# Issuing all loads and stores of a batched matmul from one queue, each store four groups behind its loads

## The chip, the cores and the metric

The kernel runs on one core of one Trainium2 chip. The metric is the device time of the whole program in microseconds (us). Executions of a kernel before scatter by under 1%, so small differences are judged by means of several runs of the same rounds.

## The reference

```python
b1, b2, m, k, n = 8, 16, 256, 512, 384
x:      float32 [8, 16, 256, 512]
weight: float32 [8, 16, 512, 384]
out = np.matmul(x, weight)          # 128 independent 256x512 @ 512x384
```

168 MB are read and 50 MB written.

## The kernel before

The 128 batches are handled in groups: 63 groups of two batches and, at the end, two groups of one. A group loads one x tile (1 MiB; the last two groups share one) and one 768 KB weight tile per batch, casts both to bf16 on VectorE (DVE), transposes x on TensorE (PE), multiplies, copies PSUM to SBUF on ScalarE (ACT) and stores 768 KB. The last two groups store 384 KB each.

```python
LAG = 3
x_pool: bufs=3    w_pool: bufs=6    out_pool: bufs=LAG + 3

def load_x(b): ... nc.sync.dma_start(x_sb[:], ...)      # SP
def load_w(b): ... nc.sync.dma_start(w_sb[:], ...)      # SP

waiting = []
def store():
    dram, out_sb = waiting.pop(0)
    nc.scalar.dma_start(out=dram, in_=out_sb)           # ACT

for n, G in enumerate(groups):
    ...                                # loads, casts, transposes of group n
    if last:
        while waiting:
            store()
    for r in range(0, RG, 2):
        ...                            # matmuls into po
        nc.scalar.copy(out=out_sb[:, r : r + 2, :], in_=po[:, :, :N])
    waiting.append((..., out_sb))
    if len(waiting) > LAG or last:
        store()
```

Instructions reach each engine in an order that the framework's scheduler chooses. In this kernel it hoists each store on ACT to directly behind its own copies, whatever LAG says. Stores on SP keep the order of the source. Each transfer reports its landing on one of eight semaphores (counters that engines wait on), used in turn, and the program issues it only after the transfer eight before it has landed.

Of the kernel before, what the change touches and what calls it, by code (L numbers as in the profile page):

```python
# [1 line left out]

# [5 lines left out]


@with_exitstack
def kernel(
    ctx: ExitStack,
    tc: tile.TileContext,
    x: bass.AP,
    weight: bass.AP,
    out: bass.AP,
):
    nc = tc.nc
    P = 128  # L20

    b1, b2, M, K = x.shape
    _, _, _, N = weight.shape
    B = b1 * b2
    KO = K // P

    x_rows = x.rearrange("b1 b2 m k -> (b1 b2 m) k")
    o_rows = out.rearrange("b1 b2 m n -> (b1 b2 m) n")
    w_flat = weight.rearrange("b1 b2 k n -> (b1 b2) k n")

    fp32 = mybir.dt.float32
    bf16 = mybir.dt.bfloat16



    GX = 2
    CX = P // GX
    R = GX * M // P


    groups = [2] * ((B - GX) // 2) + [1] * GX

    LAG = 3

    const = ctx.enter_context(tc.tile_pool(name="const", bufs=1))
    x_pool = ctx.enter_context(tc.tile_pool(name="x_pool", bufs=3))
    xb_pool = ctx.enter_context(tc.tile_pool(name="xb_pool", bufs=2))
    xt_pool = ctx.enter_context(tc.tile_pool(name="xt_pool", bufs=2))
    w_pool = ctx.enter_context(tc.tile_pool(name="w_pool", bufs=6))
    wb_pool = ctx.enter_context(tc.tile_pool(name="wb_pool", bufs=4))  # L50
    out_pool = ctx.enter_context(tc.tile_pool(name="out_pool", bufs=LAG + 3))
    psum_t = ctx.enter_context(tc.tile_pool(name="psum_t", bufs=2, space=bass.MemoryType.PSUM))
    psum_o = ctx.enter_context(tc.tile_pool(name="psum_o", bufs=3, space=bass.MemoryType.PSUM))

    identity = const.tile([P, P], bf16)
    make_identity(nc, identity)

    def load_x(b):
        x_sb = x_pool.tile([P, R, K], fp32, name="x_sb")
        nc.sync.dma_start(  # L60
            x_sb[:], x_rows[b * M : (b + GX) * M].rearrange("(p r) k -> p r k", r=R)
        )
        return x_sb

    def load_w(b):
        w_sb = w_pool.tile([P, KO, N], fp32, name="w_sb")
        nc.sync.dma_start(w_sb[:], w_flat[b].rearrange("(kp ko) n -> kp ko n", ko=KO))  # L67
        return w_sb

    def transpose_x(x_sb, RG):  # L70


        H = R // RG
        x_bf = xb_pool.tile([P, R, K], bf16, name="x_bf")
        x_t = xt_pool.tile([P, RG, KO, P, H], bf16, name="x_t")
        for r0 in range(0, R, 4):
            nc.vector.tensor_copy(out=x_bf[:, r0 : r0 + 4], in_=x_sb[:, r0 : r0 + 4])  # L77
            for r in range(r0, r0 + 4, 2):
                pt = psum_t.tile([P, 2, KO, P], bf16, name="pt")
                for rr in range(2):  # L80
                    for ko in range(KO):
                        nc.tensor.transpose(  # L82
                            pt[:, rr, ko, :], x_bf[:, r + rr, ko::KO], identity
                        )
                j = r % RG
                nc.vector.tensor_copy(  # L86
                    out=x_t[:, j : j + 2, :, :, r // RG], in_=pt[:]
                )
        return x_t

    waiting = []

    def store():
        dram, out_sb = waiting.pop(0)
        nc.scalar.dma_start(out=dram, in_=out_sb)

    b = 0
    for n, G in enumerate(groups):
        last = n == len(groups) - 1
        C = P // G  # L100
        RG = G * M // P
        if b % GX == 0:
            x_sb = load_x(b)
        w_sb = [load_w(b + i) for i in range(G)]
        if b % GX == 0:
            x_t = transpose_x(x_sb, RG)
        w_bf = []
        for i in range(G):
            t = wb_pool.tile([P, KO, N], bf16, name="w_bf")
            nc.vector.tensor_copy(out=t[:], in_=w_sb[i][:])  # L110
            w_bf.append(t)
        if last:
            while waiting:
                store()

        out_full = out_pool.tile([P, 2 * M // P, N], fp32, name="out_sb")
        out_sb = out_full[:, :RG]
        for r in range(0, RG, 2):
            po = psum_o.tile([P, 2, 512], fp32, name="po")
            for rr in range(2):  # L120
                for ko in range(KO):
                    for i in range(G):
                        c0 = (b % GX + i) * CX
                        nc.tensor.matmul(  # L124
                            po[i * C : (i + 1) * C, rr, :N],
                            x_t[:, r + rr, ko, c0 : c0 + CX, :],
                            w_bf[i][:, ko, :],
                            start=(ko == 0),
                            stop=(ko == KO - 1),
                        )  # L130
            nc.scalar.copy(out=out_sb[:, r : r + 2, :], in_=po[:, :, :N])  # L131
        waiting.append(
            (
                o_rows[b * M : (b + G) * M].rearrange("(p r) n -> p r n", r=RG),
                out_sb,
            )
        )
        if len(waiting) > LAG or last:
            store()
        b += G  # L140


# [1 line left out]
_INS = ['x', 'weight']  # L144
_OUTS = [((8, 16, 256, 384), 'float32')]


# [23 lines left out]
```

## Time and profile before

| | before |
|---|---|
| time, median (four runs) | 531.7 us (531.2 to 532.2) |
| span of the profiled run | 528.1 us |
| chain that ended last | 97% DMA |
| both queues' share of 16 DMA engines | 76.4% + 23.0% |
| rate in 50 to 500 us | 422 GB/s |
| last weight tile's cast starts | 521.35 us |

The span runs from the first instruction to the last; the time adds some 2 us of start and end. The DMA engines are the bound, and they are full until about 510 us. What the end looks like is shown in the prediction.

### The profile page before, as it was taken

What the parts mean: (1) busy time and instruction counts of PE and PEld (TensorE: products, weight loads), DVE (VectorE), ACT (ScalarE), POOL (GpSimd) and SP (SyncE); (2) the same over time, 40 slices, a digit from 0 to 9 for tenths busy, and PEclk for the clock granted to TensorE, in tenths of its full rate; (3) what the DMA queues carried; (4) which work ended last, traced back from release to release, by engine and by line L of the source; (5) the groups of instructions that cost most, each with busy time, mean ns of one, the idle gap of its engine ahead of it and who ended that gap; (6) DMA issues with size and microseconds to landing.
All of it is one profiled execution on the core that took longest, in us unless ns stands there. A gap on an engine that the chain in (4) does not pass through costs nothing.

```text
span 528.1 us, 7363 instructions
## 1 busy us (share of the span) xinstructions
PE 343.7 (65%) x3056; PEld 234.3 (44%) x3056; DVE 277.9 (53%) x320; ACT 103.9 (20%) x129; POOL 0.7 (0%) x6
## 2 busy tenths in 40 slices
PE   4685566675766766676657667576575775766754
PEld 2454444443443544444434444354353443544432
DVE  4545545555465554555554555555555455455554
ACT  0212211221221212122112122121121211112212
POOL 0000000000000000000000000000000000000000
PEclk9969878888788887879888888898888788788889
DMA  8999999999999999999999999999999999999994
GB/s 343 399 427 422 425 421 420 427 418 423 423 419 425 421 422 424 421 423 423 421 423 421 421 424 421 422 424 422 423 419 424 422 423 422 422 422 424 422 414 192
DMA packets 37042, 218.59 MB, mean 414 GB/s; under 512 B 4113, under 2 KB 4113, under 8 KB 28817
## 3 DMA queue, kind: packets, MB, share of 16 engines
q1 hardware_dynamic: 27648, 167.78, 76.4%
q10 hardware_dynamic: 9360, 50.34, 23.0%
q8 instruction: 24, 0.39, 0.3%
q14 instruction: 10, 0.07, 0.0%
HBM read 167.77 MB, written 50.33 MB: 413 GB/s over the span
## 4 chain that ended last, share of the span: by engine, by line
DMA 97%; DVE 1%; PE 1%; issue 1%; SPq 0%; ACT 0%; DVEq 0%
DMA x_sb<-in_x_dram 97%; PE po L124 1%; DVE x_t L86 0%; DVE x_bf L77 0%; DVE w_bf L110 0%; SPq L60 0%; SPq L67 0%; ACT out_sb L131 0%; PE pt L82 0%; DVEq L77 0%
## 5 line engine op out<-in xcount | busy, mean ns | idle before, releaser
L124 PE MATMUL po<-w_bf,x_t 128*64 128x384 bf16 (+1 forms) x2032 | 276.4, 407 | 166.5 <-DVE w_bf L110 166.0
L124 PEld LDWEIGHTS <-x_t 128*64 128x64 bf16 (+1 forms) x2032 | 174.1, 135 | 252.6 <-DVE w_bf L110 127.6
L131 ACT COPY out_sb<-po 128x768 f32<-128x768 f32 x128 | 102.6, 802 | 420.2 <-PE po L124 415.9
L77 DVE CAST x_bf<-x_sb 128x2048 bf16<-128x2048 f32 x64 | 78.5, 1227 | 135.7 <-DMA x_sb<-in_x_dram 135.7
L110 DVE CAST w_bf<-w_sb 128x1536 bf16<-128x1536 f32 x128 | 119.8, 955 | 28.4 <-DMA w_sb<-in_weight_dram 27.9
L86 DVE COPY x_t<-pt 128x1024 bf16<-128x1024 bf16 x128 | 83.7, 696 | 80.3 <-PE pt L82 80.3
L82 PE MATMUL pt<-identity,x_bf 128*128 128x128 bf16 x1024 | 70.2, 222 | 13.8 <-DVE x_bf L77 13.6
L82 PEld LDWEIGHTS <-x_bf 128*128 128x128 bf16 x1024 | 60.1, 115 | 36.7 <-DVE x_bf L77 27.8
L131 ACT ACT_TABLE_LOAD x1 | 1.3, 1283 | 0.7 <-PEq L155 0.7
masks.py:199 POOL TENSOR_SCALAR_AFFINE_SELECT identity<-identity 128x128 bf16<-128x128 bf16 x1 | 0.3, 293 | 0.1
masks.py:197 POOL MEMSET identity<- 128x128 bf16 x1 | 0.2, 204 | 0.3 <-POOLq L155 0.3
L155 POOL MEMSET const-bfloat16-1.0<- 128x1 bf16 x1 | 0.1, 101 | 0.0
L155 POOL MEMSET const-uint8-127<- 128x1 uint8 x1 | 0.1, 101 | 0.0
L155 POOL MEMSET const-float32-0.0<- 128x1 f32 x1 | 0.1, 98 | 0.2 <-issue 0.2
L155 POOL MEMSET const-float32-1.0<- 128x1 f32 x1 | 0.1, 98 | 0.0
## 6 DMA issues: line engine op xcount, KB each, us to landing
w_sb<-in_weight_dram SPq DMA_DIRECT2D x128, 768.0 KB, 16.2
x_sb<-in_x_dram SPq DMA_DIRECT2D x64, 1024.0 KB, 16.1
out_dram<-out_sb ACTq DMA_DIRECT2D x63, 768.0 KB, 8.4
out_dram<-out_sb ACTq DMA_DIRECT2D x2, 384.0 KB, 2.3
```

What stands on the lines that cost most here:

```text
L77: nc.vector.tensor_copy(out=x_bf[:, r0 : r0 + 4], in_=x_sb[:, r0 : r0 + 4])
L82: nc.tensor.transpose(pt[:, rr, ko, :], x_bf[:, r + rr, ko::KO], identity)
L86: nc.vector.tensor_copy(out=x_t[:, j : j + 2, :, :, r // RG], in_=pt[:])
L110: nc.vector.tensor_copy(out=t[:], in_=w_sb[i][:])
L124: nc.tensor.matmul(po[i * C : (i + 1) * C, rr, :N], x_t[:, r + rr, ko, c0 : c0 + CX, :], w_bf[i][:, ko, :], start=(ko == 0), stop=(ko == K ...
L131: nc.scalar.copy(out=out_sb[:, r : r + 2, :], in_=po[:, :, :N])
L155: nc = _bacc.Bacc("TRN2", target_bir_lowering=False, num_devices=1)
```

## The change

Intent: one issuing queue with a fixed order in which the loads of a group always stand in front of the store of an earlier one, so that stores never overtake loads and enough stored work is left over to keep the DMA engines busy while the last group is computed.

```diff
-    LAG = 3
+    LAG = 4
...
-    def store():
+    def store(queue):
         dram, out_sb = waiting.pop(0)
-        nc.scalar.dma_start(out=dram, in_=out_sb)
+        queue.dma_start(out=dram, in_=out_sb)
...
         if last:
             while waiting:
-                store()
+                store(nc.sync)
...
         if len(waiting) > LAG or last:
-            store()
+            store(nc.sync)
```

`out_pool` grows from 6 to 7 buffers through `LAG + 3`.

## The prediction

> **What bounds the kernel now.** I read the page from the chain of waits outward: first what ended last, then whether that resource has any slack, then the two ends of the run, where slack can hide. The chain (part 4) leaves no doubt about the kind of bound:
>
> ```profile
> DMA 97%; DVE 1%; PE 1%; issue 1%; SPq 0%; ACT 0%; DVEq 0%
> ```
>
> 97% of the 528.1 us span is transfers. The other engines have room: PE is busy 65%, DVE 53%, ACT 20%. The queue part says how full the 16 DMA engines are, and how the two issuing queues share them:
>
> ```profile
> q1 hardware_dynamic: 27648, 167.78, 76.4%
> q10 hardware_dynamic: 9360, 50.34, 23.0%
> q8 instruction: 24, 0.39, 0.3%
> ```
>
> The columns are packets, MB and share of the time of 16 engines. q1 carries SP's loads, q10 ACT's stores. 76.4 + 23.0 + 0.3 = 99.7%. So two queues together fill the engines, and there is almost no gap for a new order to close. The windows view (us, busy time of five engines, granted clock, DMA share, GB/s) shows that this holds to about 510 us and no further:
>
> ```profile
> 50.00:500.00 450.00, 298.15 (x2665) 203.57 (x2665) 238.90 (x277) 88.63 (x111) 0.00 (x0) 0.85 1.02 422
> 510.00:515.00 5.00, 2.85 (x34) 1.86 (x32) 3.51 (x5) 0.80 (x1) 0.00 (x0) 1.00 0.95 397
> 515.00:520.00 5.00, 3.15 (x40) 2.37 (x36) 3.34 (x3) 1.60 (x2) 0.00 (x0) 1.00 0.69 279
> 520.00:525.00 5.00, 2.77 (x16) 1.48 (x16) 2.15 (x3) 1.60 (x2) 0.00 (x0) 1.00 0.29 114
> 525.00:528.10 3.10, 0.00 (x0) 0.00 (x0) 0.00 (x0) 0.00 (x0) 0.00 (x0) 0.77 0.45 178
> ```
>
> For 450 us the share is above 1 (packets of one engine overlap slightly) and the rate is 422 GB/s. Then 397, 279, 114: in the last 18 us the DMA engines run dry while the last group is computed. The timeline of ACT tells why:
>
> ```profile
> 517.10 0.80 ACT L131 COPY out_sb<-po 128x768 f32<-128x768 f32 x1 [0.50 <-PE po L124]
> 517.93 0.34 ACTq L95 DMA_DIRECT2D out_dram<-out_sb  x1
> 522.75 0.80 ACT L131 COPY out_sb<-po 128x768 f32<-128x768 f32 x1 [4.85 <-PE po L124]
> 523.58 0.34 ACTq L95 DMA_DIRECT2D out_dram<-out_sb  x1
> 524.05 0.80 ACT L131 COPY out_sb<-po 128x768 f32<-128x768 f32 x1 [0.50 <-PE po L124]
> 524.88 0.34 ACTq L95 DMA_DIRECT2D out_dram<-out_sb  x1
> ```
>
> Although the source says LAG = 3, the scheduled program issues each store directly after its own two copies (the same pattern stands at the first group: copies at 13.37 and 15.41, store at 16.24). So no stored work is left over for the end. When the last weight tile has landed (its cast starts at 521.35), nothing is queued behind it, and the last two half stores must wait for compute.
>
> **What the Trainium skill says.** "DMA: Bandwidth & Descriptors", section "Issuing engines are not separate DMA queues": transfers issued from different engines run on the same 16 DMA engines and interleave; a second issuer saves only issue time. The trace agrees: the shares above add to 99.7%, and an issue costs 0.33 us on SP. The same page, "Queues, rings and completion order": an engine takes turns between rows at packet granularity and consumes one ring in order. The trace agrees, in the time from issue to landing:
>
> ```profile
> w_sb<-in_weight_dram SPq DMA_DIRECT2D x128, 768.0 KB, 16.2
> x_sb<-in_x_dram SPq DMA_DIRECT2D x64, 1024.0 KB, 16.1
> out_dram<-out_sb ACTq DMA_DIRECT2D x63, 768.0 KB, 8.4
> ```
>
> A store on its own queue overtakes queued loads and lands in 8.4 us, a load in 16. "HBM Reference", "Specifications": a core streaming alone measures about 425 GB/s, bounded by its DMA engines; the trace has 422. Against the change, "Perfetto Trace Analysis", "DMA Optimizations", suggests one issuer for inputs and another for outputs where control flow is present; this program has no loop at run time, and nothing in the trace speaks for or against that.
>
> **The change, part by part.** No byte, copy or matmul changes. The built program has the 192 loads in the same order on SP, and the 65 stores move from ACT to SP, one behind each group's loads, starting after the loads of the fifth group. ACT keeps 128 copies.
>
> *Issue.* SP gains 65 issues of about 0.34 us = 22 us over 528 us; per group (8.25 us, 528/64) it then issues four transfers, 1.3 us. No bound. ACT loses the same 22 us and was 80% idle.
>
> *Steady state.* A transfer in this program waits until the one eight before it has landed (eight landing semaphores in turn). Four per group makes the window two groups: 2 x 3.25 MiB = 6.8 MB, at 422 GB/s 16.1 us. The window is as deep as before (six loads and two stores); only now all wait their turn in one ring, so stores should land in about 16 us instead of 8.4 and loads stay at about 16.
>
> *The new wait.* SP would stall if the store of group n-4 was not computed when its turn comes. Its turn comes when the store of group n-6 has landed, right after the last weight tile of group n-2, so two groups (16.5 us) after the last weight tile of group n-4 landed. From the last cast to the store issue the trace shows about 6.4 us (cast at 505.16, store at 511.49). Margin about 10 us, and behind it seven queued transfers. I expect zero stall from this, and none from the output buffers: group n reuses the buffer of group n-7, whose store landed more than a group earlier.
>
> *Packet rate.* In the packet records of the trace a 6144-byte packet takes a median of 234 ns as load and as store, an 8192-byte one 309 ns, whether the engines are doing loads alone or a mixture. Per engine: (16384 + 8064) x 234 ns + 8192 x 309 ns + small ones, over 16 = 520 us. That is the floor of any order. Before uses 2.05 us before the first packet, about 522 us of work on the slowest engine (slower first packets and instruction fetches make up the 2), and the rest is hole and drain.
>
> *The tail, the only place to gain.* By the packet records some engines still have loads until 521 us and all are then idle from about 522 to 524.4 us (2.4 us), with another 0.3 us between the two last half stores; the last packet ends at 526.9 and the span 1.3 us later. After the change, three full stores (1.87 us each: 786 KB at 422 GB/s) and the two half stores (0.93 each) lie behind the last weight load: 7.5 us of queued transfers. The last weight tile therefore lands about 516.5, and its compute (3.5 us from cast to last store issue, 521.35 to 524.88) plus 1.3 us to the first packet fits within the 5.6 us of the three full stores. The slowest engine then runs without a hole: 2.05 + 522 = 524.0 us, and 1.3 us of drain = 525.3 us of span, against 528.1: a gain of 2.8 us. Engines that already idled from 512 us on gain more, but the slowest one sets the end.
>
> Sum: -2.8 us (tail), 0 (steady state), up to +1 for bursts of stores alone (next paragraph), say +0.3. 532.1 - 2.5 = 529.6 us, which is 0.5% faster: within 2%.
>
> **Rivals.** (1) *Store bursts are slower than mixed traffic.* In one queue all engines do the same store at about the same time. For it: the 98 packets of stores that started with 15 or more stores and no loads active average 249 ns (median 236) against 234 to 235 in mixtures. If all 8064 store packets lost 15 ns, 8064 x 15 / 16 = 7.6 us, giving about 537. Against it: the outliers are few and the median is +2 ns (1 us). (2) *The end of each store holds the ring* until its writes are acknowledged, which the load queue filled until now. 65 x 0.2 us would be 13 us and about 542. Against it: in the first 13 us, with loads alone on one queue, the engines never idle between transfers; but that is no store. (3) *SP blocks on a store in order and the load queue drains.* Worth several per cent if it happened each group; the 10 us margin speaks against it. (4) *The engines' skew shrinks as well*: averaged over engines the idle time between 512 and 527 us is 5.7 us, so up to 3 us more gain, 526.5.
>
> **Range and chances.** The step I trust most is the full engines: nothing can gain over about 1.2%. The tail gain is solid but small; rivals 1 and 2 stretch the upper side. 526.5 to 533.5 us for 8 in 10. Faster by over 2% (below 521.5): 1%, since a span of some 519 us (the profiled run took 530.3 us for its 528.1 us of span) would undercut the packet floor. Slower by over 2% (above 542.8): 4%. Within: 95%.
>
> **What would show it.** Right: one hardware_dynamic queue of some 218 MB and about 99%; stores landing in about 16 us; SP waiting almost only for DMAs, not for ACT; 422 GB/s in 50 to 500 us; the rate staying near 420 up to a few us before the end. Wrong: a steady rate below 418 (rival 1 or 2, told apart by packet times against gaps), a wait of SP for out_sb of more than some us in sum (rival 3), or a hole before the last stores.

## More of the kernel before

The experiments ran in three sessions, each on another chip, so runs of two sessions are best compared by their ratios to the kernel before in their own session.

## The result, and the profile after

| | before | after |
|---|---|---|
| time, median of four runs each | 531.7 us | 526.88 us |
| span of the profiled run | 528.1 us | 524.1 us |
| ratio | | 0.9911 (95%: 0.989 to 0.9933) |

All ratios in this document are the mean time of one kernel's runs over that of the other's runs of the same rounds, so they are not quite the ratio of the medians quoted. The kernel is 0.9% faster, about 4.7 us: within 2% as predicted, and inside the range of 526.5 to 533.5, but at its lower edge (two of the four runs, 526.30 and 526.34, lie just below it, as does the 526.46 of a later repeat), and the gain is nearly twice the 2.5 us that was worked out.

The page after, its chain, its queues and its issues (size, median us to landing):

```profile
DMA 97%; PE 1%; DVE 1%; issue 0%; ACT 0%; SPq 0%; ACTq 0%; DVEq 0%
q1 hardware_dynamic: 37008, 218.12, 99.9%
q8 instruction: 24, 0.39, 0.3%
w_sb<-in_weight_dram SPq DMA_DIRECT2D x128, 768.0 KB, 16.0
x_sb<-in_x_dram SPq DMA_DIRECT2D x64, 1024.0 KB, 16.0
out_dram<-out_sb SPq DMA_DIRECT2D x63, 768.0 KB, 16.0
out_dram<-out_sb SPq DMA_DIRECT2D x2, 384.0 KB, 3.0
```

One ring (the queue of transfers that one issuing engine feeds: q1 is SP's, q10 ACT's) carries everything, and stores now wait their turn like loads: 16.0 us instead of 8.4. Multiply the queue shares by the spans: before 99.4% x 528.1 = 524.9 us of packet time per engine, after 99.9% x 524.1 = 523.6. The same bytes cost about 1.3 us less engine time. The packet records (the trace has the start, length and size of each packet, but not its engine), summed, say 524.98 and 523.44 us, 1.5 less. That is the part that I had not predicted.

The rest is in the tail. The windows after (us, busy time of PE, weight loads, DVE, ACT and POOL, granted clock, DMA share, GB/s):

```profile
50.00:500.00 450.00, 295.94 (x2666) 202.32 (x2668) 237.43 (x280) 88.09 (x110) 0.00 (x0) 0.86 1.01 423
510.00:515.00 5.00, 1.08 (x16) 0.93 (x16) 4.27 (x4) 0.52 (x1) 0.00 (x0) 1.00 1.00 417
515.00:520.00 5.00, 4.45 (x16) 2.08 (x16) 1.16 (x2) 1.01 (x2) 0.00 (x0) 0.66 0.64 263
520.00:524.10 4.10, 0.00 (x0) 0.00 (x0) 0.00 (x0) 0.58 (x1) 0.00 (x0) 0.81 0.37 145
```

In 510 to 515 us the engines are still full (417 against 397 GB/s before). The rate of 263 in the next window is no hole of all engines: the DMA share of 0.64 means that about ten of the 16 work there, and six have finished what is queued (see below). The timeline after shows when the last group is computed:

```profile
515.25 4.45 PE L125 MATMUL po<-w_bf,x_t 128*128 128x384 bf16 x16 [2.95 <-DVE w_bf L110]
515.55 0.96 DVE L110 CAST w_bf<-w_sb 128x1536 bf16<-128x1536 f32 x1 [0.35 <-DMA w_sb<-in_weight_dram]
517.65 0.80 ACT L132 COPY out_sb<-po 128x768 f32<-128x768 f32 x1 [7.13 <-PE po L125]
519.78 0.80 ACT L132 COPY out_sb<-po 128x768 f32<-128x768 f32 x1 [1.34 <-PE po L125]
```

The last weight tile is cast at 515.55 us instead of 521.35: three full stores (5.6 us by the prediction's 1.87 us each) now stand behind its load, not before or among the last loads. The last copy comes at 519.78 instead of 524.05, although the 16 last matmuls took 4.45 us at a granted clock of 0.66, against 2.77 before. The waits of SP after (us in total, times, longest) show the rival of a blocked SP to be small:

```profile
SPq L67 <- DMA w_sb<-in_weight_dram: 175.8, 118, 2.9
SPq L60 <- DMA x_sb<-in_x_dram: 117.9, 58, 2.1
SPq L95 <- DMA out_dram<-out_sb: 85.9, 57, 2.9
SPq L95 <- ACT out_sb L132: 14.6, 4, 7.5
```

SP waits for ACT four times only, 14.6 us in all. Between 50 and 500 us there is no such wait; all four come after 495 us, where the remaining stores have to wait for the last groups.

**The engines drift apart.** Each transfer lands in 16 parts, one per DMA engine, and the trace has the time of each, though not which engine it belongs to. That the last part is the same engine's each time is assumed here. The spread between first and last of the 16 is 0.5 us for the first load and grows with the run. In the changed kernel the last weight load has six engines within 1.0 us and the other ten 4.1 to 6.5 us behind; in the kernel before the spread of the last weight load is 9.3 us. So the end is set by the slowest engines. The last load landed at 521.3 us before and at 515.5 after, nearly all of which is the 5.6 us of stores now behind it. The drift is also larger with stores on ACT: at the 113th of the 128 weight loads the spread is 8.8, 8.4 and 8.8 us in the three kernels with stores on ACT up to the tail, and 5.0 to 6.3 us in the one-queue kernels with LAG 2 to 8. A likely reason, which no run shows, is that a slow engine serves the stores of the other ring in turn with the loads that it still has to do.

### The profile page after: what moved, and what is told of

The parts are those of the page before. It is cut to its first block, busy times and chain, and to the rows that moved or that the text cites. A ratio compares the mean times of both kernels' runs of the same rounds, so it can differ in the third digit from the quotient of the medians.

```text
span 524.1 us, 7422 instructions
## 1 busy us (share of the span) xinstructions
PE 339.3 (65%) x3056; PEld 231.8 (44%) x3056; DVE 273.4 (52%) x320; ACT 103.8 (20%) x129; POOL 0.7 (0%) x6
## 3 DMA queue, kind: packets, MB, share of 16 engines
q1 hardware_dynamic: 37008, 218.12, 99.9%
## 4 chain that ended last, share of the span: by engine, by line
DMA 97%; PE 1%; DVE 1%; issue 0%; ACT 0%; SPq 0%; ACTq 0%; DVEq 0%
DMA x_sb<-in_x_dram 94%; DMA w_sb<-in_weight_dram 3%; PE po L125 1%; DVE x_t L86 0%; DVE x_bf L77 0%; DVE w_bf L110 0%; ACT out_sb L132 0%; PE pt L82 0%; SPq L60 0%; ACTq L132 0%; DVEq L77 0%
## 5 line engine op out<-in xcount | busy, mean ns | idle before, releaser
L125 PE MATMUL po<-w_bf,x_t 128*64 128x384 bf16 (+1 forms) x2032 | 271.0, 400 | 136.3 <-DVE w_bf L110 135.9
L125 PEld LDWEIGHTS <-x_t 128*64 128x64 bf16 (+1 forms) x2032 | 171.5, 132 | 219.8 <-DVE w_bf L110 122.8
L110 DVE CAST w_bf<-w_sb 128x1536 bf16<-128x1536 f32 x128 | 116.7, 952 | 1.9 <-DMA w_sb<-in_weight_dram 1.9
```

The costliest lines, as they stand in the source:

```text
L110: nc.vector.tensor_copy(out=t[:], in_=w_sb[i][:])
L125: nc.tensor.matmul(po[i * C : (i + 1) * C, rr, :N], x_t[:, r + rr, ko, c0 : c0 + CX, :], w_bf[i][:, ko, :], start=(ko == 0), stop=(ko == K ...
```

## The experiments

Eleven runs were made, of ten further kernels and of the changed one again; all gave correct results. Theory: the gain comes from stores kept back, which fill the engines while the last group is computed (tail). First rival: it comes from the single ring in the steady stretch. Second: ACT waits of SP (LAG too short) cost time.

**Only the tail.** The stores stay on ACT, except for the last five. Against the kernel before (`store` takes its queue as in the change):

```diff
+    LAG = 4
         if last:
             while waiting:
-                store()
+                store(nc.sync)
         if len(waiting) > LAG or last:
-            store()
+            store(nc.sync if last else nc.scalar)
```

> The kernel before, except that the stores of the last five groups (three full, two half) are issued from SP behind the last weight load; all other stores stay on ACT, right behind their copies. Theory (tail): the gain comes from stores kept back to fill the DMA engines while the last group is computed. Then this has most of it: 2.5 to 3.5 us under before (528 to 529), rate near 420 GB/s up to about 514 us, one hole of about 1 us before the last half store, steady rate and store landing time (8.4 us) as before. Rival (one ring): the gain comes from the single ring in the steady stretch. Then this stays within 0.7 us of before (531 to 532).

Measured 529.08 us (528.21 to 531.86, six runs), ratio 0.9949 (0.9916 to 0.9983): 2.7 us of gain by the ratio, just over half of the whole and within the 2.5 to 3.5 that the tail theory said. The profiled run was the slowest of the six (531.86). Its timeline shows what went wrong in the end:

```profile
514.75 4.12 PE L124 MATMUL po<-w_bf,x_t 128*64 128x384 bf16 x30 [0.22 <-DVE w_bf L110]
518.80 1.09 PE L82 MATMUL pt<-identity,x_bf 128*128 128x128 bf16 x16
521.84 1.80 DVE L110 CAST w_bf<-w_sb 128x1536 bf16<-128x1536 f32 x2
525.65 0.80 ACT L131 COPY out_sb<-po 128x768 f32<-128x768 f32 x1 [0.50 <-PE po L124]
```

With no stores between them the last loads came faster than the last groups were computed. The two last weight tiles are cast together at 521.84 though the landing records have the last of them at 517.3, because the transposes waited for slow matmuls of the group before. The five stores were not enough to cover that.

**Only the steady stretch.** The complement: against the changed kernel, only the last five stores go to ACT.

```diff
             while waiting:
-                store(nc.sync)
+                store(nc.scalar)
...
-            store(nc.sync)
+            store(nc.scalar if last else nc.sync)
```

> The complement: stores of the groups up to the last five on SP four groups behind as in the changed kernel, but the last five issued from ACT right behind their own copies, so that none is kept back. Tail theory: 0.5 to 1.5 us under before (530.2 to 531.2), with the hole of 2 to 3 us before the last half stores back. Rival (one ring): nearly the whole gain, 527 to 528.

Measured 530.90 us (530.12 to 531.84), ratio 0.9978 (0.9949 to 1.0008): 1.2 us of gain by the mean, which the interval does not tell from none. The hole before the last half stores is back, from 522 to 524 us in the trace (DMA share and rate are the last two columns):

```profile
505.00:510.00 5.00, 2.75 (x19) 1.63 (x18) 3.21 (x4) 0.00 (x0) 0.00 (x0) 0.50 1.05 393
510.00:515.00 5.00, 3.02 (x27) 2.00 (x23) 0.40 (x1) 1.60 (x2) 0.00 (x0) 0.86 0.96 324
522.00:524.00 2.00, 1.65 (x7) 0.49 (x5) 0.94 (x1) 0.80 (x1) 0.00 (x0) 0.50 0.00 0
```

So taking the tail away takes most of the gain away. But this kernel carries a handicap of its own, which the experiment doesn't separate: where the stores change over to ACT the engines are busy (share 1.05) and yet move only 393 GB/s. By the packet records the 6144- and 8192-byte packets from 505 to 514 us take 1.5 us per engine more than their usual 234 and 309 ns, against 0.01 us in the changed kernel. Why is not known. Without it the steady stretch might show up to 1.5 us more gain than 1.2.

**LAG 3 and LAG 6** (one constant of the changed kernel, which sets only how many full stores stand behind the last load: 2, 3 and 5 for LAG 3, 4 and 6).

```diff
-    LAG = 4
+    LAG = 3      # and, in the other kernel, 6
```

> The changed kernel with LAG 3 instead of 4: one full store less (1.87 us) behind the last load, the ring is as single as before. Tail theory: the hole before the last half store grows from about 1 to about 2.5 us, time 1 to 2 us above the changed kernel (528 to 529). Rival (one ring): as the changed kernel, 526.5 to 527.3.

> The changed kernel with LAG 6: two full stores more behind the last load. Tail theory: the hole of about 1 us closes, no idle engine time on the slowest engine, 0.3 to 0.8 us under the changed kernel (526.1 to 526.6); further lag would add nothing. Rival (one ring): as the changed kernel, 526.5 to 527.3. Another rival: a longer lag hurts at the start or through buffers, above 527.5.

LAG 3: 529.59 us (528.44 to 530.17), 0.9948. LAG 6: 525.66 us (525.22 to 525.77), 0.9876. The steady rate of both is 423 GB/s, as with LAG 4, which fits the tail theory, though a step of 1 GB/s there would be about 1 us, so that the rate alone doesn't show smaller differences. LAG 3 lost 2.0 us against LAG 4 by the ratios and 2.7 by the medians, at or over the upper end of the 1 to 2 expected; LAG 6 gained 1.9 by the ratios and 1.2 by the medians, more than the 0.3 to 0.8 expected. The windows of LAG 6 show the engines full while the last group is computed:

```profile
510.00:515.00 5.00, 2.77 (x16) 1.40 (x16) 2.00 (x3) 1.60 (x2) 0.00 (x0) 1.00 1.02 420
515.00:520.00 5.00, 0.00 (x0) 0.00 (x0) 0.00 (x0) 0.00 (x0) 0.00 (x0) 0.59 0.81 334
520.00:525.00 5.00, 0.00 (x0) 0.00 (x0) 0.00 (x0) 0.00 (x0) 0.00 (x0) 0.50 0.21 82
```

All compute is over before 515 us, at 420 GB/s, and the rest is stores draining from the ring. The scatter between runs shrinks too, from 1.7 us at LAG 3 to 0.6. One thing in my expectations was misread: the hole of 1 us at LAG 4 is one of most engines. By the landing records the last engine was through with the first half store at 522.05 us and with the last half store at 522.98, 0.93 us later. A half store is 8 packets of some 123 ns on each engine, about 1 us, so if both are the same engine it had practically no hole in that execution.

**The tail with seven stores.** If all of the gain were tail, the two-queue kernel with as many stores kept back as LAG 6 (five full ones and the two half ones) should equal it. One line against the first experiment:

```diff
-    LAG = 4
+    LAG = 6
```

> As the first experiment (stores on ACT behind their copies, the last ones from SP behind the last weight load), but seven stores kept back instead of five. In the five-store version the last loads, with no stores between them, came faster than the last groups could be computed, and the last store came 3 to 4 us late. With five full stores (9.3 us) behind the last load that lateness should be covered. Theory (the gain is all in the tail, the single ring in the steady stretch gives nothing): within 0.7 us of the one-queue kernel with LAG 6, 525.2 to 526.4. Rival (the single ring itself gives 1 us or more in the steady stretch, as the 1.2 us of the complement hints): 526.7 to 528.

528.02 us (527.8 to 528.7), 0.9942. The theory fails here: the rival's interval (526.7 to 528) is met, at its edge. With the tail covered, the two-queue kernel is still 2.4 us slower than the one-queue kernel with LAG 6 (medians of two sessions whose kernel before differs by 0.4), and as much slower than LAG 8 of its own session (525.65, see below). Its landing records show one engine 1.5 us behind the rest at the end. And its packets take longer. The queue lines of that kernel, then of LAG 6:

```profile
q1 hardware_dynamic: 28656, 172.50, 79.0%
q10 hardware_dynamic: 8352, 45.62, 20.9%
```

```profile
q1 hardware_dynamic: 37008, 218.12, 100.0%
```

99.9% x 525.9 = 525.4 us of packet time against 100.0% x 523.5 = 523.5. Where the time goes can be seen in the packet records between 50 and 500 us:

| kernel | 8192-byte packets, mean ns | above 312 ns | all packets, us per engine |
|---|---|---|---|
| before | 311.7 | 29% | 525.0 |
| tail only, five / seven stores | 311.9 / 312.0 | 29% / 31% | 525.0 / 525.1 |
| after (two profiles) | 309.6 / 309.4 | 1.5% / 1.5% | 523.4 / 523.6 |
| LAG 2, 3, 5, 6, 8 | 309.7 to 310.0 | 1.7 to 3.3% | 523.6 to 524.3 |
| steady stretch only | 309.8 | 1.5% | 525.2 |
| LAG 1 | 322.4 | 11% | 560.4 |

The last column is of the whole run. So with stores on a queue of their own nearly a third of the x packets is delayed by some ns, in every kernel that has it. Over 8192 x packets and 16 engines, the 2.1 ns between before and after make 1.1 us; the whole sums differ by 1.5. Two rows warn against reading the sum as a cost of the second queue alone: the steady-stretch kernel has fast x packets and still a sum of 525.2, because of the slow packets from 505 to 514 us, and at LAG 1, with one queue only, packets take longer where SP holds the next transfers back.

**The changed kernel again, LAG 8 and LAG 1**, with the previous kernel in one session.

> The changed kernel itself once more, as the reference for the lag series on this chip. 526.3 to 527.9 as in its four runs on record; ratio to before 0.989 to 0.993.

> The changed kernel with LAG 8. Tail theory: the hole is already closed at LAG 6, so nothing more: 525.2 to 526.0. If more stores kept back gave more by themselves (rival: the longer the lag the better), under 525.

> The changed kernel with LAG 1: the store of the group before stands behind each group's loads, so SP waits for its compute (about 6.4 us after its last weight tile landed) while about 8.2 us of transfers are queued. This is the edge of the wait that was predicted to be harmless at LAG 4. If the margin reckoning is right, SP waits for ACT in nearly every group, some 6 us each, and the engines run dry only now and then: 530 to 545. If SP's wait is much more costly than reckoned: over 560. If it is no matter at all: 529 to 531 (only the tail hole of before).

The changed kernel: 526.46 us, 0.9916. LAG 8: 525.65 us (525.57 to 525.78), 0.9896: nothing beyond LAG 6, as the tail theory says. LAG 1: 601.57 us, 1.1327, far over the expected 530 to 545 and in the branch "much more costly than reckoned". SP's wait for ACT is as long as reckoned, 427.2 / 65 = 6.6 us each:

```profile
SPq L95 <- ACT out_sb L132: 427.2, 65, 11.7
```

```profile
50.00:500.00 450.00, 295.30 (x2344) 195.03 (x2342) 210.24 (x245) 77.55 (x97) 0.00 (x0) 0.77 0.95 371
```

(The first fence is SP's waits, the second the windows view, both of LAG 1.) What failed is the reckoning of what covers it: 8.2 us of queued transfers against 6.6 us of mean wait (longest 11.7), plus the issue of the next loads and the time to their first packet (0.85 us from an issue at 523.58 to the first packet at 524.43 in the kernel before). Each group takes 1.1 us longer: 601.6 / 64 = 9.4 us instead of 8.3. Of the 75 us over LAG 4, 37 are in packets that take longer (560.4 against 523.6 us per engine), and the other half in gaps (a DMA share of 0.95).

**LAG 2 and LAG 5, and x on the other queue.** The third kernel asks whether any second ring makes packets slow, or stores on it:

```diff
     def load_x(b):                    # against LAG 6
-        nc.sync.dma_start(
+        nc.scalar.dma_start(
```

> The changed kernel with LAG 2. SP still waits for ACT in most groups, but about 16 us of transfers are queued then instead of 8, so the engines should not run dry: steady rate 422 to 423 GB/s as at LAG 3, and only the tail is worse by one full store (1.9 us) than LAG 3: 530 to 532. If one group of lag is lost to the wait as at LAG 1 (rate below 415 in the steady stretch): over 540.

> The changed kernel with LAG 5: four full stores (7.5 us) behind the last weight load against some 5 to 6.5 us from its landing to the first packet of the last half store. Tail theory: the hole is closed or nearly so, 525.4 to 526.2, and less scatter between runs than LAG 4. Otherwise as LAG 4, 526.3 or more.

> The one-queue kernel with LAG 6, but the x loads issued from ACT: two queues again, with the stores kept back at the end all the same and with no store on the second queue. Theory (a second ring in use makes packets slower, 29 to 31% of the 8192-byte packets above 312 ns in the kernels with stores on ACT, 1.5 to 3% in those with one queue): 25% or more of the 8192-byte packets above 312 ns here too. Rival (it is stores cutting in between loads of the other ring that slows them): under 10%. The time can also suffer from x loads standing behind waiting copies on ACT; it is not the measure here: 526 to 535.

LAG 5: 525.83 us (525.64 to 525.87), 0.9881, as expected, with a scatter of 0.2 us where LAG 4 has 2.2 (525.99 to 528.22). LAG 2: 529.33 us (528.54 to 530.05), 0.9945, 0.7 us under the expected range and the same as LAG 3. Its waits and its steady window:

```profile
SPq L95 <- ACT out_sb L132: 278.0, 65, 8.9
```

```profile
50.00:500.00 450.00, 296.33 (x2687) 202.97 (x2685) 235.43 (x278) 89.55 (x112) 0.00 (x0) 0.86 1.01 423
```

SP waits 278 us for ACT, 4.3 us each time, and the rate does not move: about 16 us of transfers (two groups) are queued when such a wait begins. The same kind of wait, 6.6 us each, cost 70 us against the kernel before at LAG 1. That LAG 2 is no worse than LAG 3, which the tail theory did not expect, stays open. In the trace of LAG 3 the end was held up by matmuls at a low clock (5.97 us for the 32 of the last full group and 5.30 for the 16 of the last, against 2.77 for those 16 in the kernel before), so that the landing of the last load alone did not set it.

x on ACT: 525.15 us (525.12 to 525.51), below the expected 526 to 535, and 0.9871, not told apart from LAG 6 (0.9876). 12.9% of its 8192-byte packets are above 312 ns, between the two expectations, so neither is met: the x packets are slower here too (mean 311.1 ns), but the 6144-byte ones are a little faster (234.9 against 235.7 ns at LAG 6), and the sum of all packets is 523.4 us per engine, as low as with one ring. So a second ring as such costs nothing here; the higher sums go with stores on it. By what mechanism is not shown.

The lag series together (one queue; "kept back" is the full stores behind the last weight load, and the landing time is that of the last two half stores, 2.3 us when nothing is queued ahead of them):

| LAG | kept back | time, us | ratio | half stores land in |
|---|---|---|---|---|
| 1 | 0 | 601.57 | 1.1327 | 2.3 us |
| 2 | 1 | 529.33 | 0.9945 | 2.3 us |
| 3 | 2 | 529.59 | 0.9948 | 2.7 us |
| 4 (the change) | 3 | 526.46 | 0.9916 | 3.6 us |
| 5 | 4 | 525.83 | 0.9881 | 4.2 us |
| 6 | 5 | 525.66 | 0.9876 | 7.9 us |
| 8 | 7 | 525.65 | 0.9896 | 10.8 us |

LAG 5, 6 and 8 beat both kernels. In one session, no run of LAG 8 is above 525.78 us and none of LAG 4 under 525.99. The last microsecond is bought with one or two 6 KB output buffers per partition.

## Why the prediction was right or wrong

The class and the range were right, and so was the tail as the larger part of the gain; that it is "the only place to gain" was not. The range held in part by luck: its lower edge had been set for a shrinking skew of the engines (rival 4), and what took the time there was in part packet time, which the prediction had ruled out as a gain. By its steps:

- **Full engines, no gain over about 1.2%: held for the change.** 97% DMA before and after; the best kernel is 1.3% faster.
- **Stores land in about 16 us, SP waits almost only for DMAs: right** (16.0 us; 14.6 us for ACT). The 14.6 us are more than the "some us in sum" that was to show rival 3, but all are at the end, where no load is left to hold up.
- **Rate near 420 GB/s up to a few us before the end: missed.** It is 417 to 515 us and 263 after, because six engines are early. The reckoning was for the slowest engine and left out how far the engines are apart.
- **The tail, -2.8 us: right in kind, near in size.** The spans differ by 4.0 us, of which 1.5 are packet time, so 2.5 are tail. The tail-only kernel gives 2.7, with seven stores 3.1. Two of its readings were off: by the packet records one engine worked to 522.68, so that the hole on the slowest engine was about 1.75 us and not 2.4, and from an issue to its first packet it is 0.85 us, not 1.3. The measured tail is thus more than the slowest engine's holes (1.75 + 0.3 us); the smaller drift (rival 4) may be the rest. The three full stores were to cover the compute of the last group on the slowest engine. In the profiled execution they just did, with matmuls at a clock of 0.66, but all 16 engines finished the last half store within 0.2 us of each other, so most had been waiting for it: there was no reserve. The second profile of this kernel has the same 16 matmuls at full clock (2.77 instead of 4.45 us), 1.2 us between first and last engine in the last half store, and the same time, 526.34 us: the slower matmuls were just hidden. LAG 5 and 6 are 0.6 to 0.8 us faster by the medians and scatter much less. That the slower executions of LAG 4 had a hole is likely, but no trace of one was taken.
- **The steady stretch, 0 to +1, entered as +0.3: this term was mis-sized, and its sign was wrong.** It measured -1.5 us of packet time over the whole run, about 1.0 of it between 50 and 500 us and 0.6 in the first 20 (excess over 234 and 309 ns). I took the median packet (234 and 309 ns) as the same with one queue and with two; the medians are, but 29% of the 8192-byte packets were above 312 ns with stores on ACT, and 1.5% after. The mean would have shown room below the 524.9 us.
- **Rival 1 (store bursts are slow) and rival 2 (a store holds the ring): fell.** Packet time went down and the steady rate is 423 GB/s. The 98 packets that spoke for rival 1 had up to one load running beside them; with none there were two, of 234 ns. The 0.2 us of rival 2 rest on no run.
- **Rival 3 (SP blocks): fell at LAG 4, and is real at LAG 1,** where the time is 70 us above the kernel before.
- **Rival 4 (the skew shrinks): partly.** The last weight load's spread went from 9.3 to 6.5 us; how much of the time that is worth was not separated.

The split of the 4.7 us by experiments (2.7 to 3.1 tail, about 1.2 steady) adds up within their intervals of 1.3 to 1.8 us to each side, and with the handicap of the steady-stretch kernel no sharper split is shown. Why the ten engines fall behind the six stays open.

## What to carry to other kernels

In a kernel that is bound by DMA all the way, look at what is queued behind the last load: keep back as many stores as cover the compute of the last group, and issue them in order behind it. A queue that blocks on compute was harmless here where the transfers queued ahead lasted well longer than each wait: about 16 us against waits of 4.3 us at LAG 2, which left the steady rate as it was, and not where they were about as long: 8.2 us against a mean of 6.6 and a longest of 11.7 at LAG 1. Before calling a median packet time a floor, look at the mean and at the share of slow packets, and remember that packet times also grow where transfers are held back (LAG 1).

## What the Trainium skill lacked or had wrong

- "Perfetto Trace Analysis", "DMA Optimizations": it suggests separate issuers for inputs and outputs, "especially" with loops or control flow. In this kernel without either, moving all to one issuer was faster (0.9911), and keeping loads and stores apart, all but the last seven stores, was slower (528.02 against 525.66 us).
- "DMA: Bandwidth & Descriptors", "Issuing engines are not separate DMA queues": it says that a second issuer only saves issue time. Here it also decides which transfer comes first (a store lands in 8.4 us or in 16.0), as the turn-taking that the prediction cites from the same page implies, and stores from a second queue went with slower packets (29% against 1.5% of the 8192-byte packets above 312 ns, 525.0 against 523.4 us per engine). With x loads in place of stores on the second queue that sum stayed at 523.4.
- In no page: how far the 16 engines drift apart under an evenly split load from SP and ACT, from 0.5 us of spread in the first load to 6.5 us (one queue) or 9.3 us (stores on their own queue) in the last weight load, in two sets of six and ten at the end of the changed kernel. At LAG 1, where the engines run short of transfers in each group, it is only 1.1 us there.
